# Output projection in one PSUM tile per output block, the state read ahead of the solve, and a longer fill behind one DMA round trip

## The chip, the cores and the metric

The kernel runs on one core of a Trainium2 chip. The metric is the device time of one launch, in microseconds: before the change three runs gave 1146.88, 1148.94 and 1152.93, median 1148.94. The engines are PE (matmul), DVE (vector), ACT (scalar), POOL, and SP, which only issues DMAs here. Each runs its own queue strictly in the order in which the program was laid down.

## The reference, cut to what matters

One decoder layer on 544 tokens (512 of a prompt, 32 of eight sample requests of four tokens), model width 1024, all in float32:

```
x = layer_norm(ALPHA*x + 0.5*swiglu(x, ffn1))
proj = x @ w_in                       # RWKV columns and convolution columns
r, k, v, decay, a, kk = f(proj)       # 8 heads of 64
S <- S diag(w) + (S(-kk))(kk*a)^T + v k^T ;  o = S r        # per token
y_rwkv = group_norm(o)... * g ;  y_conv = c_b * depthwise_conv(c_c*c_h)
x = layer_norm(ALPHA*x + concat(y_rwkv, y_conv) @ w_out)
x = layer_norm(ALPHA*x + 0.5*swiglu(x, ffn2))
```

Outputs are the two x parts, the new recurrence state and the shift and convolution states. `concat(y_rwkv, y_conv) @ w_out` is the output projection: 1024 inputs, in eight blocks of 128 (0 and 1: the first four heads, 2 and 3: the last four heads, 4 to 7: the convolution).

## The kernel before, in words

**Layout.** Activations lie transposed: features on the 128 partitions, tokens along the free axis, in halves h = 0 (tokens 0 to 255) and h = 1 (256 to 543). A large product is exact to nearly float32 by three fast products: each operand is split into a high part (ACT copies it, line 133) and a low part (DVE subtracts, line 134), and `mm3` issues high x high, high x low, low x high (lines 149 to 151), 256 or 288 columns each, into one PSUM tile named `mm`, of which there are three. The recurrence's small products are plain float32, 64 columns, into five PSUM tiles named `sm`.

**Weights.** `wload` takes a raw tile, issues its DMA on SP, and splits it into an `hl` tile. Raw and `hl` tiles come from rings in strict rotation. While the output projection runs, the `hl` ring has four slots (three of its own and one extra, `w4`), the raw ring two. A new load may be split into its slot only when the last matmul that reads the slot's earlier weights is done.

**Recurrence.** The heads form two groups, g = 0 and g = 1. Tokens go in eight chunks of 64. `elim(g)` inverts the chunks' small triangular matrices: DVE rounds on 16x16 blocks, a round trip through DRAM (tiles `De`, `Dd`, `DM`), then small matmuls (line 929). `chain(g)` then takes the eight chunks one after another. A step is: SC times the state S (line 977), copied to W by ACT (979); XT times W (984), copied to UV by DVE and ACT (985, 986); BK times UV (991), added into the next state by four DVE operations (1000, 1002); and the output, S times AR (1009) plus UV times SC (1013), both into one `sm` tile, copied to O by ACT (1015). `sample(g)` does the same for the sample tokens.

**What sets the order.** The critical work is a generator that yields a number where it must wait; `weave` then draws that many units (times a factor per stage, the table FILL) of background work from a queue `bg`: matmuls of other products. Then a list scheduler of the framework, with its own idea of durations, lays down each engine's queue. The order on the chip is fixed; a row that waits blocks all rows behind it on its engine.

**Around the change.** The fill of `elim(1)`, of `chain(1)` and of what follows is, in this order: the last convolution block (`conv_last`, weights `in_win`), the output projection's inputs 4 to 7, 0 and 1 for h = 0 (`wout(0)`, weights `wo_c` and `wo_0`), then inputs 2 and 3 (`last(0)`, weights `wo_1`). Then `wout(1)` and, behind it, `last(1)`; beside them run the group norm of the last heads and the layer norm of half 0 (`layer_norm`, lines 194 to 231), and then the second FFN starts.

Of the kernel before, what the change touches and what calls it, by code (L numbers as in the profile page):

```python
# [15 lines left out]
OP = mybir.AluOpType  # L16
# [5 lines left out]
KD = D // P  # L22
# [5 lines left out]
T = TP + NSEQ * TS  # L28
# [27 lines left out]
def R(par):  # L56
    return slice(64 * par, 64 * par + 64)
# [4 lines left out]
def body(ctx: ExitStack, tc: tile.TileContext, xT, gu1, wd1, win, wo_c, wo_0, wo_1, gu2, wd2, lora, w0, vec, cst,  # L62
         sst, cstate, s0, y_o, wkvp_o, wkvs_o, shift_o, conv_o):
    nc = tc.nc
    PE, ACT, DVE, POOL = nc.tensor, nc.scalar, nc.vector, nc.gpsimd
# [12 lines left out]
    xhl = keep.tile([P, 2, KD, T], F32R, name="xhl")  # L78
# [10 lines left out]
    def big():  # L89
        return ps.tile([P, 512], F32, name="mm", bufs=3)  # L90

    def sm():
        return ps.tile([P, 512], F32, name="sm", bufs=5)
# [15 lines left out]
    def wtiles():  # L109
        return raw_tile(), hl_tile()  # L110

    def wload(src, n=1024, parts=1):
        raw, hl = wtiles()
        m = n // parts
        for i in range(parts):
            dma(raw[:, i * m:i * m + m], src[:, i * m:i * m + m])
            wsplit(hl, raw, i * m, i * m + m)
        return hl
# [23 lines left out]
            hl, i = hl[i // 4], i % 4  # L142
        return hl[:, j, i * P:(i + 1) * P]

    def mm3(out, hl, src, ks, c0, c1, off=0):
        n = len(ks)
        for i, k in enumerate(ks):
            wh, wl = (block(hl, j, off + i) for j in range(2))
            PE.matmul(out, wh, src[:, 0, k, c0:c1], start=(i == 0), stop=False)  # L149
            PE.matmul(out, wh, src[:, 1, k, c0:c1], start=False, stop=False)  # L150
            PE.matmul(out, wl, src[:, 0, k, c0:c1], start=False, stop=(i == n - 1))  # L151
            if i % 2 and i < n - 1:
                yield 6 * ((c1 - c0) / 2.4 + 3)

    bg = deque()
# [467 lines left out]
    z = pool(zst, "zp").tile([P, KD, T], F32, name="z")  # L623
# [6 lines left out]
    raw, hl = wtiles()  # L630
# [244 lines left out]
    def elim(g, mid=None):  # L875
        AR = ARs[g]
        est = ExitStack()
        ep = pool(est, f"elim{g}")
        AT = ep.tile([P, 16, 16], F32, name="AT")
        De = ep.tile([P, 16, 16], F32, name="De")  # L880
        tm = ep.tile([P, 64], F32, name="tm")
        dma(AT, diag(Ad))
        POOL.memset(De, 0.0)
        POOL.memset(De.rearrange("p a b -> p (a b)")[:, 0:256:17], 1.0)
        for pl in range(2):
            for par in range(2):
                sc = SC[R(par), pl, par, 0:8, 0:64]
                DVE.tensor_tensor(sc, sc, offm[R(par), None, :].to_broadcast([64, 8, 64]), op=OP.mult)
        yield 3000
        for k in range(15):  # L890
            n = 15 - k
            tv = tm[:, :n * (k + 1)].rearrange("p (i j) -> p i j", j=k + 1)
            DVE.tensor_tensor(tv, AT[:, k, k + 1:16, None].to_broadcast([P, n, k + 1]),
                              De[:, k, None, 0:k + 1].to_broadcast([P, n, k + 1]), op=OP.mult)
            DVE.tensor_tensor(De[:, k + 1:16, 0:k + 1], De[:, k + 1:16, 0:k + 1], tv, op=OP.add)
            yield 400
        DVE.tensor_copy(AT, De.rearrange("p a b -> p b a"))
        dma(diag(Dd[0]), De)
        dma(diag(Dd[1]), AT)
        for d, x in zip(Dd, (DM[:, 0:8], DT)):  # L900
            for par in range(2):
                dma(x[R(par)].rearrange("p c d t -> p (c d) t"), d[par, :, 0:64].rearrange("c s t -> s c t"))
        est.close()
        if mid is not None:
            mid()
        yield 6000
        pieces = (range(0, 4), range(4, 8), range(8, 9))
        for rnd in range(4):
            for x in pieces:
                sam = x[0] == 8  # L910
                m = (64, 64, 32, 16)[rnd]
                j0 = (0, 16, 32, 48)[rnd]
                nn = (64, 48, 32, 16)[rnd]
                if sam:
                    m, j0, nn = 32, 0, 32
                q = sm()
                for c in x:
                    for pl in range(2):
                        for par in range(2):
                            r0 = 64 * par  # L920
                            pr = slice(r0, r0 + (32 if sam else 64))
                            o = ((c - x[0]) * 2 + pl) * nn
                            lhs = DM[pr, c, pl, 0:m] if rnd else SC[pr, pl, par, c, 0:m]
                            rhs = (DM if rnd == 0 else DT if rnd == 1 else XT) if not sam else XT
                            if sam and rnd < 2:
                                rhs = ident[pr, 0:32]
                            else:
                                rhs = rhs[pr, c, pl, j0:j0 + nn]
                            PE.matmul(q[r0:r0 + m, o:o + nn], lhs, rhs, start=True, stop=True)  # L929
                cc = slice(x[0], x[-1] + 1)  # L930
                qv = q[:, :2 * nn * len(x)].rearrange("p (c d t) -> p c d t", c=len(x), d=2)
                if rnd == 0:
                    for pr in (slice(0, 32), slice(64, 96)) if sam else (slice(0, P),):
                        ACT.activation(DM[pr, cc, :, 0:nn], qv[pr], AF.Copy)
                    yield 300
                    continue
                if rnd == 1 and not sam:
                    DVE.tensor_copy(XT[:, cc, :, 0:16], DT[:, cc, :, 0:16])
                    DVE.tensor_tensor(XT[:, cc, :, 16:64], qv, DT[:, cc, :, 16:64], op=OP.add)
                    yield 300  # L940
                    continue
                for par in range(2):
                    pr = slice(64 * par, 64 * par + m)
                    dst = XT[pr, cc, :, j0:j0 + nn]
                    if sam:
                        DVE.tensor_tensor(dst, qv[pr], ident[pr, None, None, 0:32].to_broadcast([32, 1, 2, 32]), op=OP.add)
                    elif par:
                        ACT.copy(dst, qv[pr])
                    else:
                        DVE.tensor_copy(dst, qv[pr])  # L950
                yield 300
            if rnd == 0:
                for pl in range(2):
                    for par in range(2):
                        POOL.tensor_copy(SC[R(par), pl, par, 0:8, 0:64], AR[R(par), pl, 0:8, 0, :])
# [4 lines left out]
    def chain(g, cp):  # L960
        S = Sn = None
        tl = cp.tile
        AR = ARs[g]
        for c in range(8):
# [5 lines left out]
            for pl in range(2):  # L970
                for par in range(2):
                    dst = q[R(par), pl * 64:pl * 64 + 64]
                    if c == 0:
                        o = R(1 - par)
# [3 lines left out]
            W = tl([P, 2, 64], F32, name="W", bufs=2)  # L978
            ACT.activation(W, v2(q), AF.Copy)
            yield 1000  # L980
            q = sm()
            for pl in range(2):
                for par in range(2):
# [5 lines left out]
            for pl in range(2):  # L989
                for par in range(2):  # L990
                    PE.matmul(q[R(par), pl * 64:pl * 64 + 64], BK[:, pl, par, c, :], UV[:, pl, par, c, :],
                              start=True, stop=True)
# [3 lines left out]
            for par in range(2):  # L996
                dst = Sn[R(par), :, par, :] if c < 7 else SF[R(par)]
                src = v2(q, R(par))
                if c:
                    DVE.tensor_tensor(dst, S[R(par), :, par, :], src, op=OP.add)  # L1000
                    src = dst
                DVE.tensor_tensor(dst, src, pe[R(par)], op=OP.mult)
            if c == 7:
                dma(wkvp_o[:, 2 * g:2 * g + 2, :], SF)
            q2 = sm()
            if c:
                for pl in range(2):
                    for par in range(2):
                        PE.matmul(q2[R(par), pl * 64:pl * 64 + 64], S[R(par), pl, par, :], AR[R(par), pl, c, 1, :],
                                  start=(pl == 0), stop=False, skip_group_check=True)  # L1010
            for pl in range(2):
                for par in range(2):
                    PE.matmul(q2[R(par), pl * 64:pl * 64 + 64], UV[:, pl, par, c, :], SC[:, pl, par, c, 64:128],
                              start=(c == 0), stop=True, skip_group_check=True)
            ACT.activation(O[:, :, c, :], v2(q2), AF.Copy)
            S = Sn
# [212 lines left out]
    z = pool(ctx, "zp2", "right").tile([P, KD, T], F32, name="z")  # L1229
# [13 lines left out]
    def ysplit(k, y, c0, c1):  # L1243
        split(xhl[:, 0, k, c0:c1], xhl[:, 1, k, c0:c1], y[:, c0:c1])
# [22 lines left out]
    def wout(h):  # L1267
        c0, c1 = HALF[h]
        if h == 0:
            ys = [(k, yload(k)) for k in (0, 1)]  # L1270
            for k in range(KD):
                ACT.activation(z[:, k], z[:, k], AF.Identity, scale=ALPHA, bias=rb[:, k:k + 1])
        for src, n, ks in ((wo_c, 2, (4, 5, 6, 7)), (wo_0, 4, (0, 1))):
            for m in range(KD // n):
                if h == 0 and n == 2 and m == 2:
                    for k, y in ys:
                        ysplit(k, y, 0, T)
                w = wload(src[m])
                for d in range(n * m, n * m + n):
                    o = big()  # L1280
                    yield from mm3(o[:, :c1 - c0], w, xhl, ks, c0, c1, (d - n * m) * len(ks))
                    zz = z[:, d, c0:c1]
                    DVE.tensor_tensor(zz, zz, o[:, :c1 - c0], op=OP.add)
                    yield 6 * 120

    def last(h):
        c0, c1 = HALF[h]
# [132 lines left out]
```

## Time and profile before

| | |
|---|---|
| runs | 1146.88, 1148.94, 1152.93 us |
| the profiled execution, its own time | 1144.4 us |
| its span, first to last instruction | 1142.3 us |
| mean granted PE clock | 0.992 |
| PE, DVE, ACT, POOL busy | 1106.8, 857.2, 586.1, 174.2 us |
| elim(1) up to its first matmul | about 601 to 629 us of the span |
| chain(1) | about 648 to 703 us |
| wout(1) and last(1) | about 712 to 749 us |

PE is busy for 97% of the span, but a busy PE is not a full one: matmuls are pipelined, each is shown with its whole latency (some 0.3 us), and consecutive ones start 0.12 to 0.13 us apart where nothing disturbs them. What a stage of PE work costs is therefore read from starts, and from the waits.

### The profile page before, as it was taken

Reading aid. Unit: us, or ns where it says so; the run is one execution under the profiler, and the core shown is the slowest. Engines: PE = TensorE matmul, PEld = TensorE weight load, DVE = VectorE, ACT = ScalarE, POOL = GpSimd, SP = SyncE. Lnnn points to the kernel's source line nnn. Section 1 sums busy time; section 2 is a strip of 40 time slices with the busy share of each in tenths; the row PEclk is TensorE's granted clock in tenths of the full one; section 3 lists DMA queues with packets and bytes.
Section 4 is the critical chain, followed back from the end, with each engine's and each line's share of the span. In section 5 each row is a group of like instructions: output and inputs, shape, how many; then the busy total and the mean of one; then the engine's idle time right before and its main releaser. Section 6 shows DMA issues by size and latency. Waiting matters only on the chain.

```text
span 1142.3 us, 22932 instructions
## 1 busy us (share of the span) xinstructions
PE 1106.8 (97%) x9300; PEld 1049.3 (92%) x9300; DVE 857.2 (75%) x1602; ACT 586.1 (51%) x1066; POOL 174.2 (15%) x282
## 2 busy tenths in 40 slices
PE   8999999999999999999999999899999999999995
PEld 7999999999999999898788878899999999999995
DVE  7677988879776867745577368988979888787755
ACT  6545555564553476553245343657555555545523
POOL 0021131312100032221011100001222212121000
PEclk9999999999999999999999999999999999999998
DMA  8557594957742242262128423353675949577302
GB/s 281 119 112 168 131 219 116 200 149 166 163 145 78 92 132 66 53 121 78 48 66 223 118 76 96 130 184 63 130 180 124 228 97 217 148 161 167 105 1 79
DMA packets 97626, 149.32 MB, mean 131 GB/s; under 512 B 35056, under 2 KB 58992, under 8 KB 97520
## 3 DMA queue, kind: packets, MB, share of 16 engines
q1 hardware_dynamic: 70320, 111.67, 32.3%
q0 software_dynamic: 27200, 36.18, 20.2%
q8 instruction: 73, 1.20, 0.4%
q14 instruction: 33, 0.27, 0.1%
HBM read 129.17 MB, written 9.75 MB: 122 GB/s over the span
## 4 chain that ended last, share of the span: by engine, by line
PE 68%; DMA 10%; DVE 10%; issue 7%; ACT 5%; SPq 0%; ACTq 0%; POOL 0%; POOLq 0%; DVEq 0%
PE mm L149 7%; PE mm L464 7%; PE mm L151 7%; PE mm L465 6%; PE mm L466 6%; PE mm L150 6%; DMA raw<-in_gu 6%; PE sm L464 5%; PE sm L466 5%; PE sm L465 5%; DVE hl L134 2%; ACT hl L133 2%; PE sm L929 1%; DMA z<-in_xT 1%; PE sm L208 1%
## 5 line engine op out<-in xcount | busy, mean ns | idle before, releaser
L134 DVE TENSOR_TENSOR hl<-raw,hl 128x1024 fp32r<-128x1024 f32 (+3 forms) x228 | 269.5, 1189 | 67.0 <-ACT hl L133 64.8
L133 ACT ACTIVATE hl<-raw 128x1024 fp32r<-128x1024 f32 (+3 forms) x228 | 231.5, 1027 | 86.2 <-DVE raw L431 32.5
L149 PE MATMUL mm<-xhl,hl 128*128 128x256 f32 (+1 forms) x768 | 235.6, 307 | 8.4 <-ACT xhl L137 4.9
L151 PE MATMUL mm<-xhl,hl 128*128 128x256 f32 (+1 forms) x768 | 227.8, 298 | 1.4 <-DVE hl L134 1.4
L150 PE MATMUL mm<-xhl,hl 128*128 128x256 f32 (+1 forms) x768 | 226.4, 295 | 0.6 <-DVE xhl L231 0.3
L149 PEld LDWEIGHTS mm<-xhl,hl 128*128 128x128 f32 x768 | 147.4, 192 | 16.6 <-ACT xhl L137 5.2
L150 PEld LDWEIGHTS mm<-xhl,hl 128*128 128x128 f32 x768 | 147.5, 192 | 6.5 <-issue 1.6
L151 PEld LDWEIGHTS mm<-xhl,hl 128*128 128x128 f32 x768 | 147.0, 192 | 5.8 <-DVE hl L134 2.4
L464 PE MATMUL sm<-xhl,hl 128*128 128x272 f32 x432 | 124.7, 289 | 0.0
L466 PE MATMUL sm<-xhl,hl 128*128 128x272 f32 x432 | 124.6, 289 | 0.0
L465 PE MATMUL sm<-xhl,hl 128*128 128x272 f32 x432 | 124.6, 288 | 0.0
L464 PE MATMUL mm<-tv,hl 128*128 128x272 f32 x288 | 83.7, 291 | 3.5 <-ACT cpb L525 2.9
L466 PE MATMUL mm<-tv,hl 128*128 128x272 f32 x288 | 83.6, 290 | 0.0
L465 PE MATMUL mm<-tv,hl 128*128 128x272 f32 x288 | 82.5, 286 | 0.0
L466 PEld LDWEIGHTS sm<-xhl,hl 128*128 128x128 f32 x432 | 81.6, 189 | 0.0
L443 POOL DMA_DIRECT2D raw<-in_wd x32 | 39.3, 1494 | 277.2 <-DVE hlb L138 275.4
L465 PEld LDWEIGHTS sm<-xhl,hl 128*128 128x128 f32 x432 | 81.3, 188 | 0.0
L464 PEld LDWEIGHTS sm<-xhl,hl 128*128 128x128 f32 x432 | 81.3, 188 | 0.0
L437 POOL DMA_DIRECT2D raw<-in_gu x36 | 43.4, 1206 | 238.4 <-DVE hlb L138 131.7
L464 PEld LDWEIGHTS mm<-tv,hl 128*128 128x128 f32 x288 | 54.1, 188 | 5.0 <-ACT cpb L525 3.5
L464 PE MATMUL mm<-hhl,hl 128*128 128x272 f32 x192 | 57.0, 302 | 1.7 <-ACT sv L570 1.6
L464 PE MATMUL sm<-hhl,hl 128*128 128x272 f32 x192 | 55.9, 291 | 0.0
(367 smaller groups left out, 2818.9 us busy)
## 6 DMA issues: line engine op xcount, KB each, us to landing
raw<-in_gu SPq DMA_DIRECT2D x86, 512.0 KB, 5.0
raw<-in_gu POOLq DMA_DIRECT2D x36, 512.0 KB, 7.4
raw<-in_wd SPq DMA_DIRECT2D x32, 512.0 KB, 4.8
raw<-in_win SPq DMA_DIRECT2D x26, 512.0 KB, 3.6
raw<-in_wd POOLq DMA_DIRECT2D x32, 256.0 KB, 6.5
raw<-in_wd SPq DMA_DIRECT2D x16, 384.0 KB, 3.3
z<-cpb POOLq DMA_DIRECT2D x16, 272.0 KB, 8.7
z<-sv POOLq DMA_DIRECT2D x16, 272.0 KB, 5.7
```

Source lines behind the costliest of these rows:

```text
L133: ACT.activation(hl[:, 0, a:b], raw[:, a:b], AF.Copy)
L134: DVE.tensor_tensor(hl[:, 1, a:b], raw[:, a:b], hl[:, 0, a:b].bitcast(F32), op=OP.subtract)
L149: PE.matmul(out, wh, src[:, 0, k, c0:c1], start=(i == 0), stop=False)
L150: PE.matmul(out, wh, src[:, 1, k, c0:c1], start=False, stop=False)
L151: PE.matmul(out, wl, src[:, 0, k, c0:c1], start=False, stop=(i == n - 1))
L208: PE.matmul(v[:, :n], ones, qq[:, i, :], start=(j == 0 and i == 0), stop=(j == 3 and i == 1))
L437: POOL.dma_start(x.rearrange("p (s c) -> p s c", s=2), bass.AP(tensor=a11.tensor, offset=a11.offset, ap=[[2 * D, P], [P * 2 * D, 2], [1, 5 ...
L443: POOL.dma_start(four(x)[:, i], bass.AP(tensor=a11.tensor, offset=a11.offset, ap=[[DFF, P], [P * DFF, 2], [1, 256]]), accum_op=OP.add)
L464: PE.matmul(out, wh, src(0, i), start=(first and i == 0), stop=False, skip_group_check=True)
L465: PE.matmul(out, wh, src(1, i), start=False, stop=False, skip_group_check=True)
L466: PE.matmul(out, wl, src(0, i), start=False, stop=(i == n - 1), skip_group_check=True)
L929: PE.matmul(q[r0:r0 + m, o:o + nn], lhs, rhs, start=True, stop=True)
```

## The change

Three edits.

1. In `chain`, the four products S times AR of a step stand ahead of XT times W, and their `sm` tile is taken there. Before, they stood behind the state update.
2. In `wout`, one PSUM tile per output block d takes the convolution inputs (12 matmuls) and inputs 0 and 1 (6 matmuls); before, they were two groups in two passes over d, each with a DVE addition into z. The weights are loaded in the order wo_0[0], wo_c[0], wo_c[1], wo_0[1], wo_c[2], wo_c[3]; before, the four wo_c came first. The splits of inputs 0 and 1 stand ahead of all products; before, in the middle. `mm3` gets arguments that leave the accumulation open, and then also yields behind its last pair.
3. In `elim`, the wait behind the round trip through DRAM draws 15000 units for g = 1; before, 6000. The stage's factor is 0.392.

```diff
-    def mm3(out, hl, src, ks, c0, c1, off=0):
+    def mm3(out, hl, src, ks, c0, c1, off=0, start=True, stop=True):
...
-            PE.matmul(out, wh, src[:, 0, k, c0:c1], start=(i == 0), stop=False)
+            PE.matmul(out, wh, src[:, 0, k, c0:c1], start=(start and i == 0), stop=False)
...
-            PE.matmul(out, wl, src[:, 0, k, c0:c1], start=False, stop=(i == n - 1))
-            if i % 2 and i < n - 1:
+            PE.matmul(out, wl, src[:, 0, k, c0:c1], start=False, stop=(stop and i == n - 1))
+            if i % 2 and not (stop and i == n - 1):
                 yield 6 * ((c1 - c0) / 2.4 + 3)
...
-        yield 6000
+        yield 15000 if g else 6000
...
             ACT.activation(W, v2(q), AF.Copy)
             yield 1000
+            q2 = sm()
+            if c:
+                for pl in range(2):
+                    for par in range(2):
+                        PE.matmul(q2[R(par), pl * 64:pl * 64 + 64], S[R(par), pl, par, :], AR[R(par), pl, c, 1, :],
+                                  start=(pl == 0), stop=False, skip_group_check=True)
             q = sm()
...
-            q2 = sm()
-            if c:
-                for pl in range(2):
-                    for par in range(2):
-                        PE.matmul(q2[R(par), pl * 64:pl * 64 + 64], S[R(par), pl, par, :], AR[R(par), pl, c, 1, :],
-                                  start=(pl == 0), stop=False, skip_group_check=True)
...
-        for src, n, ks in ((wo_c, 2, (4, 5, 6, 7)), (wo_0, 4, (0, 1))):
-            for m in range(KD // n):
-                if h == 0 and n == 2 and m == 2:
-                    for k, y in ys:
-                        ysplit(k, y, 0, T)
-                w = wload(src[m])
-                for d in range(n * m, n * m + n):
-                    o = big()
-                    yield from mm3(o[:, :c1 - c0], w, xhl, ks, c0, c1, (d - n * m) * len(ks))
-                    zz = z[:, d, c0:c1]
-                    DVE.tensor_tensor(zz, zz, o[:, :c1 - c0], op=OP.add)
-                    yield 6 * 120
+            for k, y in ys:
+                ysplit(k, y, 0, T)
+        n = c1 - c0
+        for d in range(KD):
+            if d % 4 == 0:
+                w0 = wload(wo_0[d // 4])
+            if d % 2 == 0:
+                wc = wload(wo_c[d // 2])
+            o = big()
+            yield from mm3(o[:, :n], wc, xhl, (4, 5, 6, 7), c0, c1, (d % 2) * 4, stop=False)
+            yield from mm3(o[:, :n], w0, xhl, (0, 1), c0, c1, (d % 4) * 2, start=False)
+            zz = z[:, d, c0:c1]
+            DVE.tensor_tensor(zz, zz, o[:, :n], op=OP.add)
+            yield 6 * 120
```

What the change makes of the queues is shown at the three places of which the prediction speaks. Line numbers from 985 on are up to six higher in the changed kernel: 984, 991, 1000, 1002 and 1009 before are 990, 997, 1006, 1008 and 985 now; 1283 (the addition into z) is 1285, 1294 is 1296.

**PE where elim(1) waits for its round trip.** DM is the tile that the DRAM round trip fills; the wide rows (lines 149 to 151) are fill. Before:

```order
L150 MATMUL mm<-xhl,hl 128x256
L929 MATMUL sm<-DM,SC 64x64 x2
L929 MATMUL sm<-cs,SC 32x32 x4
L151 MATMUL mm<-xhl,hl 128x256
L149 MATMUL mm<-xhl,hl 128x256
```

Now:

```order
L151 MATMUL mm<-xhl,hl 128x256
L929 MATMUL sm<-DM,SC 64x64
L149 MATMUL mm<-xhl,hl 128x256
L150 MATMUL mm<-xhl,hl 128x256
L151 MATMUL mm<-xhl,hl 128x256
L149 MATMUL mm<-xhl,hl 128x256
L150 MATMUL mm<-xhl,hl 128x256
L151 MATMUL mm<-xhl,hl 128x256
L929 MATMUL sm<-DM,SC 64x64
L149 MATMUL mm<-xhl,hl 128x288
L929 MATMUL sm<-DM,SC 64x64 x30
```

The run of 256-column fill ahead of the first row that reads DM has 26 matmuls before and 42 now, and six more stand between the two rows that wait for the two halves of DM. From the first line-929 row to the first of chain(1) there are 6 runs of fill before and 14 now; in chain(0) 28 before and 24 now, in chain(1) 35 and 33; from the start of chain(0) to the layer norm of half 0, 87 and 89.

**PE in a step of chain(0)**, one piece of the difference (S and AR name this step's two operands of the moved product):

```order
 L151 MATMUL mm<-xhl,hl 128x288
 L977 MATMUL sm<-S,SC 64x64
-L149 MATMUL mm<-xhl,hl 128x288
+L985 MATMUL sm<-AR_4703,S 64x64
 L977 MATMUL sm<-S,SC 64x64 x3
-L150 MATMUL mm<-xhl,hl 128x288
-L151 MATMUL mm<-xhl,hl 128x288
-L149 MATMUL mm<-xhl,hl 128x288
-L984 MATMUL sm<-W,XT 64x64 x4
```

The moved product takes the place of a single fill matmul between the first row of line 977 and the three others.

**PE and ACT in wout(1), at the step from output block 3 to 4.** hl_8385 is wo_0[0], hl_8532 is wo_c[2]; mm_8492 and mm_8536 are the PSUM tiles of blocks 3 and 4. PE now:

```order
L151 MATMUL mm_8492<-xhl_68,hl_8385 128x288
L149 MATMUL mm_8536<-xhl_68,hl_8532 128x288 [waits Activation_49]
L150 MATMUL mm_8536<-xhl_68,hl_8532 128x288
L151 MATMUL mm_8536<-xhl_68,hl_8532 128x288 [waits DVE_49]
L149 MATMUL mm_8536<-xhl_68,hl_8532 128x288
```

ACT now (hl_8527 is wo_0[1], hl_8589 is wo_c[3], lnr the layer norm's square root):

```order
L133 ACTIVATE hl_8527<-raw_8526 128x1024 [waits DMAHW2_49]
L1098 ACTIVATE gq1_8380<-gq1_8380 128x288 [waits Activation_49]
L137 ACTIVATE xhl_68<-O_4697 128x288 [waits DVE_49]
L133 ACTIVATE hl_8532<-raw_8531 128x1024 [waits DMAHW3_49,PE_49]
L137 ACTIVATE xhl_68<-O_4697 128x288 [waits DVE_49]
L133 ACTIVATE hl_8589<-raw_8588 128x1024 [waits DMAHW4_49]
L218 ACT_TABLE_LOAD
L218 ACTIVATE lnr_7089<-sm_8512,eps_69 128x256 [waits PE_49]
```

wo_c[2] is the fifth load and so falls into the slot of the first, wo_0[0], which block 3 still reads; its split waits for PE, and PE's next row waits for the split. Before, the fifth load was wo_0[0] and its slot held wo_c[0], read last in block 1.

## The prediction, on record before the result

> **What bounds the kernel now.** I read the page's chain of waits first, then PE's waits, then the stretches in which the granted clock falls, then PE, ACT and DVE in order of time around the edits.
>
> ```profile
> span 1142.3 us, 22932 instructions
> PE 1106.8 (97%) x9300; PEld 1049.3 (92%) x9300; DVE 857.2 (75%) x1602; ACT 586.1 (51%) x1066; POOL 174.2 (15%) x282
> PE 68%; DMA 10%; DVE 10%; issue 7%; ACT 5%; SPq 0%; ACTq 0%; POOL 0%; POOLq 0%; DVEq 0%
> ```
>
> PE is the bound nearly everywhere, so fill that only moves from one place to another changes nothing; an edit counts by the PE time that it empties or fills. PE's waits, by releaser, whole span, then 700 to 760 us alone (us in total, times, longest):
>
> ```profile
> PE sm L929 <- DMA DM<-Dd: 2.3, 1, 2.3
> ...
> PE mm L149 <- DVE z L1283: 1.9, 2, 1.4
> PE mm L149 <- ACT hl L133: 0.9, 1, 0.9
> PE mm L151 <- DVE hl L134: 0.6, 1, 0.6
> ```
>
> The first is the round trip of elim(1), the other three (3.4 us) are wout(1) and last(1). Each place is followed by a stretch at half clock, whose rows show PE, PEld, DVE, ACT and POOL busy, then the granted clock:
>
> ```profile
> 626.50:629.10 2.60, 0.34 (x3) 0.13 (x2) 0.04 (x1) 0.38 (x1) 2.12 (x8) 1.00 1.26 201
> 629.80:633.25 3.45, 3.45 (x18) 3.45 (x17) 0.00 (x0) 0.43 (x2) 0.00 (x0) 0.51 1.28 241
> 736.80:742.40 5.60, 3.12 (x19) 2.35 (x18) 5.60 (x13) 2.60 (x5) 0.00 (x0) 1.00 0.00 0
> 742.50:745.90 3.40, 3.40 (x17) 3.40 (x16) 2.08 (x5) 0.36 (x1) 0.00 (x0) 0.50 0.79 257
> ```
>
> 3.4 us at half clock does 1.7 us of work, so each costs 1.7 us. In both cases some 2 us of idle came just before. The third thing to see is that changing between fill and small products costs:
>
> ```profile
> 608.63 0.29 PE L151 MATMUL mm<-xhl,hl 128*128 128x288 f32 x1
> 608.76 0.30 PE L149 MATMUL mm<-xhl,hl 128*128 128x288 f32 x1
> ...
> 656.25 0.28 PE L150 MATMUL mm<-xhl,hl 128*128 128x256 f32 x1
> 656.47 0.33 PE L977 MATMUL sm<-S,SC 128*64 128x64 f32 x2
> 656.73 0.38 PE L151 MATMUL mm<-xhl,hl 128*128 128x256 f32 x1
> 657.04 0.45 PE L977 MATMUL sm<-S,SC 128*64 128x64 f32 x6
> ```
>
> Undisturbed fill starts every 0.13 us (288 columns; 0.12 for 256). From 656.25 to 657.04 stand two fills, worth 0.24, and two small records at about 0.05: 0.34 of work in 0.79 us, with two changes to small and one back. I take 0.3 us for a run of fill between small products.
>
> **Edit 3, the longer fill.** Now 42 instead of 26 fills of 256 columns stand ahead of the first row that reads DM: 16 x 0.12 = 1.9 us more. The wait was 2.3. DVE's last rows ahead of the round trip now leave two fill operations behind themselves:
>
> ```profile
> 619.12 0.41 DVE L1153 TENSOR_TENSOR cu<-cc,mm 128x256 f32<-128x256 f32 x1
> 619.45 0.18 DVE L1155 TENSOR_TENSOR cu<-cc,mm 128x32 f32<-128x32 f32 x1
> 619.55 0.17 DVE L895 TENSOR_TENSOR De<-De,tm 128x15 f32<-128x15 f32 x1
> ```
>
> That brings De forward by some 0.4 us. 1.9 + 0.4 covers the 2.3: **-2.3** (bounds -1.9 and -2.5), and the half clock behind it goes: **-1.7** (bounds 0 and -1.7). What is late next is nothing: the six fills between the two waiting rows cover the second half of DM. If the fill were gone, the wait would be back whole.
>
> The Trainium skill (TensorE: Matmul & The Clock Gate, Part 1: The HAM clock gate) says that the clock falls after at least one idle window of about 3.4 us and comes back after a busy one. The trace agrees on the length of the slow stretch, 3.4 us, and differs on its cause: 2.3 us of wait was enough. By the page's rule the wait would not explain the half clock, and -1.7 would be 0.
>
> **Edit 1, the moved product.** No instruction is added: 28 matmuls per group move. They wait for S, as line 977 does, so no new wait; queued behind them on PE is XT times W, which waits for ACT's W anyway:
>
> ```profile
> 657.58 0.28 ACT L979 ACTIVATE W<-sm 128x128 f32<-128x128 f32 x1 [1.16 <-PE sm L977]
> ```
>
> Four of them (0.4 us, eight records at 0.05) fit into W's 0.3 us and its handover. Their `sm` tile is held one solve longer, with five tiles for it; I cost that at nothing, and at most at one drain of 0.3 us per step, 2 us, if the tiles run out. What counts is the runs of fill: 4 fewer in chain(0), 2 fewer in chain(1), 8 more in the small products of elim(1), 2 more in all around: +2 x 0.3 = **+0.6** (bounds -1.8, the chains' alone, and +2.4, elim's alone).
>
> **Edit 2, the DVE additions.** Sixteen additions of about 0.37 us (the spacing behind the 0.4 us that a row shows) leave DVE:
>
> ```profile
> L1283 DVE TENSOR_TENSOR z<-z,mm 128x288 f32<-128x288 f32 x16 | 7.1, 446 | 0.7 <-PE mm L151 0.7
> L134 DVE TENSOR_TENSOR hl<-raw,hl 128x1024 fp32r<-128x1024 f32 x7 | 8.4, 1218 | 0.0
> ```
>
> In wout(0) they lie beside PE's work and are worth nothing. In wout(1) they are the 1.9 us of PSUM waits: a tile lasts 18 fills (2.4 us) instead of 6 (0.8), and DVE's lag no longer reaches PE. The 0.9 is of the same sort, since DVE was held by ACT, which was held by a load:
>
> ```profile
> 731.76 1.06 ACT L133 ACTIVATE hl<-raw 128x1024 fp32r<-128x1024 f32 x1 [1.33 <-DMA raw<-in_wo]
> ...
> 733.25 0.48 DVE L231 SCALAR_TENSOR_TENSOR xhl<-z,vc,xhl 128x256 fp32r<-128x256 f32 x1 [1.00 <-ACT xhl L230]
> 733.65 0.45 DVE L1283 TENSOR_TENSOR z<-z,mm 128x288 f32<-128x288 f32 x1
> ```
>
> So the tail's 3.4 us of waits go: **-3.4**, and its half clock with them, -1.7.
>
> **Edit 2, the ring.** Here a wait is added. wo_c[2] takes the slot of wo_0[0], read until block 3 ends, and block 4 needs it at once. PE stands for ACT's split and its handover, less what two matmuls on the high part cover, then for DVE's low part: 0.3 of drain + 1.06 + 1.22 - 0.3 = **+2.3** in wout(1) (bounds 1.1, the high part alone, and 2.6). In wout(0) the same split stands in ACT's queue ahead of the chain's UV copy, and PE has only the rows behind that copy left: 1.06 + 0.26 + 0.2 = **+1.5** (bounds 0.3, if other rows cover all but the copy, and 2.6). How such a split delays the copy shows already:
>
> ```profile
> 695.85 1.06 ACT L133 ACTIVATE hl<-raw 128x1024 fp32r<-128x1024 f32 x1 [2.31 <-PE mm L151]
> 696.93 0.26 ACT L986 COPY UV<-sm 64x128 f32<-64x128 f32 x1
> ```
>
> Behind the split in wout(1) are queued another split, a table load and the layer norm's root:
>
> ```profile
> 724.97 1.28 ACT L218 ACT_TABLE_LOAD   x1
> 726.28 0.48 ACT L218 ACTIVATE lnr<-sm,eps 128x256 f32<-128x256 f32 x1
> 727.44 1.74 DVE L219 RECIPROCAL lnr<-lnr 128x256 f32<-128x256 f32 x1
> ```
>
> The root moves from 0.4 to some 5 us behind the variance sums, and all of DVE's normalizing (16 operations at 0.4, the reciprocal, five additions) stands ahead of the low split of last(1)'s first weights. Added up from these rows, that split ends 15.7 us behind the variance sums; PE, with 84 fills at 0.13 and the 2.3 us stall, arrives at 13. PE has 6 fills for the difference: **+1.9** (bounds 0 and 3). I expect one stall of the three to bring a half clock: **+1.7** (bounds 0 and 5.1); two earlier waits of 0.9 and 0.6 brought none by themselves.
>
> **Edit 2, the input splits.** Lines 1240 and 137 move ahead. Splits of y stand in ACT's queue ahead of a W copy, behind a transfer:
>
> ```profile
> y<-ycd SPq DMA_DIRECT2D x2, 272.0 KB, 3.1
> 673.29 0.64 ACT L137 ACTIVATE xhl<-y 128x544 fp32r<-128x544 f32 x1
> ```
>
> Issue to landing 3.1 plus two splits is 4.4 us; PE has about 4.8 us of rows (12 fills, 24 small records, the 512-column sample product, three changes) until it needs W: **0** (bounds 0 and 1.4, a slow landing). Nor does SP delay them: the weight load ahead finds its raw tile free.
>
> **Sum.** -2.3 - 1.7 + 0.6 - 3.4 - 1.7 + 2.3 + 1.5 + 1.9 + 1.7 = **-1.1 us**, against the profiled execution: span 1142.3 to 1141.2, its own time 1144.4 to 1143.3. That execution lies 4.5 us under the median of the three runs, 1148.94; the sum applied to it gives **1147.8**. A measurement of this kernel tells some 0.5% (5.7 us) from no change: the forecast is no change.
>
> **Rivals.**
>
> *The waits go and none comes* (faster). If the ring's splits are covered, the sum is -2.3 - 1.7 + 0.6 - 3.4 - 1.7 = -8.5, 1140.4. For it: every wait named is in the rows, and ACT is idle half the time. Against it: block 4 needs the slot that block 3 has just read, and no row stands between.
>
> *The ring's stalls bring half clock each* (slower). Where each of the three stalls empties PE for 1.5 us or more inside one of the clock's windows, all three pay 1.7, 3.4 more than in the sum, and with the upper bounds of the two ring stalls (2.6 each, +1.4) and of last(1) (3, +1.1) the result is -1.1 + 3.4 + 1.4 + 1.1 = +4.8, 1153.7; it is slower than before as soon as two stalls do. For it: 2 us of idle did so twice. Against it: 0.9 did not.
>
> *Half clock has nothing to do with the waits* (the page's rule). Both slow stretches stay and none is added: -1.7 is struck twice and +1.7 once, -1.1 + 3.4 - 1.7 = +0.6, 1149.5. For it: nothing but two stretches are there to judge by. Against it: each stands right behind the idle.
>
> *The longer fill does nothing*, since the fills wait for their own weights or DVE is late: 4.0 us are not won, +2.9, 1151.8. Against it: PE is dense up to 626.5.
>
> **How the numbers follow.** Chances: the forecast 0.52, all covered 0.20, stalls with half clock 0.12, clock apart 0.08, fill idle 0.08. The forecast's own range is 1143 to 1152. The whole range takes in the covered case and the slower one, **1140 to 1153.5**. Faster by over 0.5% (under 1143.2): the covered case and a little of the forecast, 0.24. Slower by over 0.5% (above 1154.7): the upper half of the slower case and part of the idle fill, 0.09. Within: 0.67.
>
> **What would show it.** Right: PE's wait for DM under 0.4 us with clock 1.00 behind it; PSUM waits on the addition gone; PE waiting for ACT L133 and DVE L134 at block 4, 1 to 2.6 us each; the root some 5 us behind the variance sums. Wrong: no PE wait at block 4 (the ring is covered, faster), or a wait for DM that stays.

## The result, and the profile after

Four runs of the changed kernel took 1130.86 to 1137.86 us, median **1134.97 us**; four runs of the kernel before beside them had a median of 1147.91. The ratio is **0.9884, 95% interval 0.9849 to 0.9919**: faster by 1.2%, where the prediction said no change (1147.8) and its range ended at 1140.

The page of the changed kernel, in the lines that answer to those of before:

```profile
span 1134.5 us, 22909 instructions
PE 1099.5 (97%) x9300; PEld 1045.3 (92%) x9300; DVE 851.6 (75%) x1586; ACT 586.2 (52%) x1066; POOL 172.6 (15%) x282
PE 64%; DVE 11%; DMA 10%; issue 9%; ACT 5%; POOL 0%; SPq 0%; ACTq 0%; POOLq 0%; DVEq 0%
```

PE is the bound as before. PE's waits of the changed kernel at the places of which the prediction spoke, out of the list for the whole span (us in total, times, longest):

```profile
PE mm L151 <- DVE hl L134: 1.4, 2, 0.8
PE mm L149 <- DVE z L1285: 0.9, 1, 0.9
PE sm L929 <- DMA DM<-Dd: 0.5, 2, 0.3
PE mm L149 <- DVE z L1296: 0.5, 1, 0.5
...
PE mm L149 <- ACT hl L133: 0.2, 1, 0.2
```

The wait for DM fell from 2.3 to 0.5 us, and the tail's waits are about 2 us (0.9, 0.6 of line 151's 1.4, 0.5). No row shows the two stalls at output block 4 that the prediction added.

Waits alone don't make 13 us. Two quantities worked out from trace and runs are used from here on. **Time beside the fill** of a stage is its elapsed time less what its fill would take undisturbed (0.1325 us per fill of 288 columns, 0.1185 per fill of 256, the spacing of such rows); it doesn't change when fill only moves from one stage to another. **At full clock** means less the time lost to half clock: for a stage half the length of the half-clock stretches in it, for a run span times mean granted clock. In us, beside the fill and at full clock, one profile of each kernel:

| stage | before | edit 1 alone | edit 2 alone | edit 3 alone | all three |
|---|---|---|---|---|---|
| chain(0) | 30.5 | 27.5 | 30.5 | 30.5 | 27.5 |
| elim(1) up to the first row that reads DM | 17.9 | 14.9 | 18.1 | 16.3 | 13.6 |
| elim(1)'s small products behind it | 9.8 | 9.7 | 9.6 | 11.6 | 12.1 |
| chain(1) | 32.8 | 30.5 | 32.6 | 30.4 | 31.4 |
| tail: variance sums of half 0 to layer norm of half 1 | 6.7 | 6.7 | 6.0 | 6.5 | 4.9 |
| the rest of the region | 12.1 | 11.8 | 12.1 | 11.7 | 11.5 |

The first two columns and the last say where time was saved: in the steps of chain(0), whose only edit is the moved product, in elim(1) up to DM, and in chain(1). The prediction gave this edit +0.6. Differences of half a microsecond are not to be read: two profiles of the changed kernel differ by up to 0.6 in a stage.

For the stages as the view of stretches shows them, chain(0), the head of elim(1), chain(1) and the tail, before and then with edit 1 alone (window, length, then PE, PEld, DVE, ACT, POOL busy, granted clock, DMA share, GB/s):

```profile
525.30:569.10 43.80, 43.80 (x505) 33.19 (x506) 21.36 (x57) 9.82 (x31) 3.31 (x12) 1.00 0.18 62
579.90:589.80 9.90, 9.66 (x92) 7.97 (x91) 7.28 (x17) 2.83 (x8) 0.71 (x4) 1.00 0.39 102
651.40:703.40 52.00, 52.00 (x571) 40.63 (x571) 36.89 (x90) 21.46 (x52) 3.21 (x10) 1.00 0.27 84
724.40:750.20 25.80, 22.29 (x142) 20.69 (x141) 22.94 (x49) 12.57 (x19) 0.00 (x0) 0.93 0.42 143
```

```profile
526.50:566.10 39.60, 39.24 (x496) 30.83 (x495) 21.53 (x56) 10.63 (x31) 3.29 (x12) 1.00 0.19 60
577.50:585.40 7.90, 7.34 (x93) 6.34 (x92) 7.40 (x16) 2.78 (x8) 0.70 (x4) 1.00 0.39 81
646.30:696.10 49.80, 49.66 (x572) 38.77 (x571) 36.28 (x89) 21.68 (x52) 3.19 (x10) 1.00 0.28 87
716.90:740.90 24.00, 20.70 (x142) 19.12 (x140) 22.78 (x49) 12.22 (x18) 0.00 (x0) 1.00 0.45 154
```

Chain(0) is 4.2 us shorter with 11 fills less in it (1.4 us of fill that went elsewhere); PE is busy all of the 43.8 us before, so no list of waits could show this.

### The profile page after: what moved, and what is told of

It reads as the page before. It is cut to its first block, busy times and chain, and to the rows that moved or that the text cites. A ratio compares the mean times of both kernels' runs of the same rounds, so it can differ in the third digit from the quotient of the medians.

```text
span 1134.5 us, 22909 instructions
## 1 busy us (share of the span) xinstructions
PE 1099.5 (97%) x9300; PEld 1045.3 (92%) x9300; DVE 851.6 (75%) x1586; ACT 586.2 (52%) x1066; POOL 172.6 (15%) x282
## 4 chain that ended last, share of the span: by engine, by line
PE 64%; DVE 11%; DMA 10%; issue 9%; ACT 5%; POOL 0%; SPq 0%; ACTq 0%; POOLq 0%; DVEq 0%
PE mm L149 7%; PE mm L464 7%; PE mm L466 6%; PE mm L465 6%; PE mm L151 6%; PE mm L150 6%; DMA raw<-in_gu 5%; PE sm L464 4%; PE sm L466 4%; PE sm L465 4%; DVE hl L134 3%; ACT hl L133 2%; PE sm L929 1%; DMA raw<-in_wd 1%; PE sm L208 1%
```

## The experiments

All twelve kernels were timed in five rounds, four to a comparison, each against the kernel before in the same comparison. Means at full clock (span times mean granted clock), and the time lost to half clock, with twice the standard error:

| kernel | runs | ratio, 95% interval | at full clock, us | lost to half clock, us |
|---|---|---|---|---|
| before, three comparisons | 68 | | 1135.5 ± 0.5 | 13.0 ± 1.0 |
| edit 1 | 6 | 0.9889 (0.9853 to 0.9926) | 1127.9 ± 1.5 | 7.8 ± 2.1 |
| edit 2 | 12 | 0.9980 (0.9952 to 1.0009) | 1134.6 ± 1.1 | 11.5 ± 2.4 |
| edit 3 | 12 | 0.9939 (0.9917 to 0.9962) | 1134.3 ± 1.1 | 8.5 ± 1.2 |
| edits 1 and 2 | 12 | 0.9904 (0.9875 to 0.9934) | 1127.8 ± 0.5 | 10.4 ± 2.4 |
| edits 1 and 3 | 6 | 0.9911 (0.9889 to 0.9934) | 1126.2 ± 0.9 | 10.6 ± 2.3 |
| edits 2 and 3 | 11 | 0.9916 (0.9889 to 0.9942) | 1132.9 ± 0.8 | 7.4 ± 1.6 |
| all three, with the first comparison | 10 | 0.9879 (0.9844 to 0.9914) | 1126.5 ± 1.3 | 7.3 ± 1.6 |
| ring forced | 6 | 0.9861 (0.9824 to 0.9897) | 1124.8 ± 1.6 | 7.9 ± 1.2 |
| before, grouped | 12 | 1.0003 (0.9982 to 1.0024) | 1135.1 ± 0.7 | 11.7 ± 2.0 |
| all three, apart | 12 | 1.0037 (1.0011 to 1.0062) | 1142.7 ± 1.1 | 8.6 ± 3.0 |
| all three, prefetch | 6 | 0.9896 (0.9872 to 0.9920) | 1126.6 ± 1.3 | 8.5 ± 1.7 |
| all three, blocks | 6 | 0.9885 (0.9852 to 0.9918) | 1124.8 ± 1.2 | 10.2 ± 1.7 |

The ratio of "all three" is that of the later comparison alone. Of the last column, 2.4 to 4.0 us lie behind the last matmul in every profile and cost nothing, so only its differences count.

### The edits one by one

Edit 1 alone:

```diff
+            q2 = sm()                      # S times AR, ahead of XT times W
...
             for pl in range(2): ... PE.matmul(q[...], XT[R(par), c, pl, :], W[R(par), pl, :], ...)
...
-            q2 = sm()                      # ... no longer behind the state update
```

> Only the moved product S times AR (edit 1). In the two profiled executions the time that PE spends beside its wide fill (elapsed time of a stage less 0.13 us for each fill of 288 columns and 0.12 for each of 256) fell from 30.5 to 27.5 us in chain(0) and from 32.8 to 31.4 in chain(1). Theory A, changes of shape: it is edit 1 that does this, since a step's rows of 64x64 stand between rows of 128x64 less often; -3 to -5 us against before, chain(0) rest 27.5 +- 0.7, with the two waits of elim(1) and the tail still there. Theory B, the waits alone: edit 1 is worth what the prediction gave it, between -1.8 and +2.4 us; the 3 us in chain(0) came from the other edits' order, and this run's chain(0) rest stays near 30.5.

Measured: ratio 0.9889, at full clock 8.3 us under the before of the same comparison (1136.2). Chain(0) has the 27.5 us of theory A to the tenth; chain(1) is 30.5, less than expected, and elim(1) up to DM, which no theory had named, is 3.0 us shorter. Theory B falls; theory A has the right stage, and its -3 to -5 in all is too little. Edit 1 alone is worth most of what the change is worth.

Edit 2 alone (the hunks on `mm3` and `wout`), and edit 3 alone:

```diff
-        yield 6000
+        yield 15000 if g else 6000
```

> Only the output projection in one PSUM tile (edit 2). Theory A: the ring costs nothing, as in the changed kernel's trace, and the tail wins 3.5 us there; -3 to -5 us against before, no PE wait for ACT line 133 or DVE line 134 between output blocks 3 and 4; the PE wait for DM (2.3 us) stays. Theory B, the prediction's sum for this edit: -3.4 - 1.7 + 2.3 + 1.5 + 1.9 + 1.7 = +2.3 us.

> Only the longer fill behind elim(1)'s round trip (edit 3). Theory A: the wait for DM falls from 2.3 to about 0.4 us and no half clock stands behind it: -2 to -4 us, of which some is given back by the additional runs of fill between elim's small products (85 fills in 22.2 us before, 22.9 after with the half clock gone). Theory B: the wait shrinks only when all three edits stand together; -1 to +1 us.

Measured for edit 2: 0.9980, an interval that holds 1; at full clock -1.6 ± 1.4 against its comparison. The wait for DM stayed (2.6), as theory A said. At full clock the gain is under its -3 to -5, which the plain ratio's interval (-5.5 to +1.0 us) doesn't rule out; +2.3 (theory B) is out. Its PE waits from 700 to 765 us show why it is so small:

```profile
PE mm L151 <- DVE hl L134: 2.2, 1, 2.2
PE mm L149 <- DVE z L1285: 0.6, 1, 0.6
PE mm L149 <- ACT hl L133: 0.4, 1, 0.4
```

The waits for the PSUM additions went from 1.9 to 0.6, and the low split of last(1)'s first weights became 2.2 us late. That is the size of the prediction's +1.9, but not its path: the layer norm's root starts 1.4 us behind the variance sums (730.62 against 729.21), not 5. DVE's last normalizing, ahead of the low split, waited 3.05 us for ACT's rows of line 230, and ACT stood 5.23 us for a load (raw from in_gu) ahead of them.

Measured for edit 3: 0.9939; at full clock -1.9 ± 1.4, theory A's -2 to -4 within the error; the plain ratio says some -7 us, half clock included. The wait for DM is 0.8, not 0.4. It saves 1.6 us up to DM (17.9 to 16.3), and gives 1.8 back in the small products behind (9.8 to 11.6), which have 15 runs of fill among them instead of 7. The last is inside the prediction's bounds (+2.4 for these 8 runs). Chain(1) is 2.4 us shorter, which neither theory named; in program order it has 8 runs of fill fewer, 27 instead of 35. The half clock in elim's small products is gone, but this profile has one at the start of chain(1) instead (656.2 us).

### Pairs

> Edits 1 and 3 without edit 2. Over the first five comparisons, span times mean granted clock (so that stretches at half clock don't count) was, as the mean of the runs: before 1136.2, edit 1 alone 1127.9 (-8.3), edit 2 alone 1134.6 (-1.6), edit 3 alone 1134.3 (-1.9), all three 1125.3 (-10.9). Theory A, the three add: -8.3 - 1.9 = -10.2 at full clock, 1126, and 0.988 to 0.991 in the plain ratio. Theory B, edit 2 is needed for the other two to be worth all they show: -8 or less at full clock.

> Edits 1 and 2 without the longer fill. Theory A: -8.3 - 1.6 = -9.9 us at full clock; the wait for DM stands at about 1.7 us as with edit 1 alone. Theory B, overlap: -8 to -8.8.

> Edits 2 and 3 without the moved product. Theory A: -1.6 - 1.9 = -3.5 us at full clock; the two chains have 27 and 27 runs of fill and 32 and 28 direct changes of shape, against 23 and 32, 19 and 12 of the changed kernel. Theory B, the prediction's sum without its +0.6 for edit 1: -1.7 us.

> The changed kernel as it is, beside the three others of this comparison. From the single edits, in span times mean granted clock (edit 1 -8.3 us, edit 2 -1.6, edit 3 -1.9): theory A, they add, -11 to -12.5 against before. Theory B, what edit 2 and edit 3 win is the same waits that edit 1 shortens already: -8 to -9, as edits 1 and 3 together showed (-8.4).

The edits of these kernels are the hunks of the change that their names give. Measured at full clock, each against the before of its own comparison: edits 1 and 3 -8.4, edits 1 and 2 -7.8, edits 2 and 3 -2.7, all three -8.3. Without edit 1, edits 2 and 3 are worth 1.6 to 2.7 us; on top of it, within the error, nothing: theory B holds for the pairs with edit 1, and -2.7 ± 1.2 lies between the two theories for edits 2 and 3. Why the gains don't add stays open. The expectation of -11 to -12.5 for all three was wrong; the first four runs (1125.3) had been a little low. What is left of the gain in plain time, about 5 us, is less time at half clock (13.0 to 7.3). In plain time the shares are less clear: by their ratios edit 1 alone is worth some 13 us, edits 2 and 3 together some 10, all three some 14. Edits 2 and 3 get most of theirs from half clock (14.2 to 7.4 in their comparison), edit 1 from full clock.

### The ring, forced into the slot that the prediction named

One line ahead of the loop over d in `wout` puts wo_0[0] into the extra slot, which holds one tile; wo_c[2], four loads later, must follow into it:

```diff
         n = c1 - c0
+        wstate["hl"] += (3 - wstate["hl"]) % 4
         for d in range(KD):
```

> The changed kernel with one line more: before each wout the count of the weight ring is advanced so that wo_0[0] takes the extra slot, which holds one tile only; so wo_c[2], four loads later, must take wo_0[0]'s slot, as the prediction said it did. Theory A, the slot was misread but the price was right: the prediction's stalls of 2.3 us in wout(1) and 1.5 in wout(0) appear, with a half clock of 1.7 behind at least one; +3.8 to +7 us against the changed kernel, ratio to before 0.992 to 0.995. Theory B, such a split is covered whatever slot it takes: within 1 us of the changed kernel, ratio 0.988.

In the changed kernel the slot is another. The built program gives wo_0[0] the address 76992, and wo_c[1] and wo_c[2] both 85184: the pool hands out the slot that came free first, not the one that was given out first. In wout(0), too, wo_c[2] follows wo_c[1] (68800) and not wo_0[0] (85184). So the strict rotation in the description of the kernel doesn't hold for the three own slots of the `hl` ring; in the kernel before, both rules give the same slots. PE, ACT and DVE of the changed kernel at this place:

```profile
716.33 0.29 PE L151 MATMUL mm<-xhl,hl 128*128 128x288 f32 x1
716.46 1.89 PE L216 MATMUL sm<-lnq,ones 128*128 128x256 f32 x8
718.00 0.48 PE L149 MATMUL mm<-xhl,hl 128*128 128x288 f32 x1
...
718.84 0.29 PE L151 MATMUL mm<-xhl,hl 128*128 128x288 f32 x1
718.97 0.30 PE L149 MATMUL mm<-xhl,hl 128*128 128x288 f32 x1
```

```profile
716.66 1.06 ACT L133 ACTIVATE hl<-raw 128x1024 fp32r<-128x1024 f32 x1 [1.03 <-PE mm L151]
```

```profile
717.75 1.23 DVE L134 TENSOR_TENSOR hl<-raw,hl 128x1024 fp32r<-128x1024 f32 x1 [0.45 <-ACT hl L133]
```

The row at 716.33 is block 3's last on wo_c[1]. wo_c[2] is split right behind it, while PE works on the variance sums (line 216) and block 3's six rows on wo_0[0] (718.00 to 718.84); block 4 starts at 718.97 and needs the low part at its third row. Nothing waits. Forced, PE's waits from 700 to 760 us are:

```profile
PE mm L149 <- ACT hl L133: 2.0, 1, 2.0
PE mm L151 <- DVE hl L134: 1.4, 1, 1.4
PE mm L149 <- DVE z L1286: 0.2, 1, 0.2
```

So the stall in wout(1) has the predicted size, 2.0 us where 2.3 was said; in wout(0) none appears. Yet the kernel is as fast as the changed one, 0.9861. At full clock the tail is 1.6 us longer (6.5 against 4.9 beside the fill) and chain(1) 1.4 shorter (30.0 against 31.4; the scheduler, with another slot, laid three runs of fill fewer). In plain time this profile's tail is 3.3 us longer (25.6 against 22.3), for a half clock follows the stall. Both theories fall in part: the mechanism and its price in wout(1) are real, a loss of 3.8 to 7 us in all is not. Where the runs win the tail's loss back is shown only for chain(1)'s 1.4. The misread slot alone doesn't explain the miss.

### What edit 1 changes: the price of a change of shape

A step of chain(0) on PE, before:

```profile
533.30 0.30 PE L150 MATMUL mm<-xhl,hl 128*128 128x288 f32 x1
533.52 0.33 PE L991 MATMUL sm<-UV,BK 128*64 128x64 f32 x2
533.78 0.32 PE L1009 MATMUL sm<-AR,S 64*64 64x64 f32 x2
534.04 0.45 PE L991 MATMUL sm<-UV,BK 128*64 128x64 f32 x6
534.41 0.44 PE L1009 MATMUL sm<-AR,S 64*64 64x64 f32 x6
534.78 0.45 PE L1013 MATMUL sm<-SC,UV 128*64 128x64 f32 x8
```

Behind the operation stands the shape of the weights, 128*64 or 64*64. Six records of one shape and the change to the next take 0.37 us, two records and the change 0.26; so a record is 0.03 to 0.05 and a **change of shape 0.16 to 0.2 us**. Before, S times AR (64*64) stands in pieces between products of 128*64; moved, it stands beside XT times W, which is 64*64 too. Two kernels test this.

The first keeps the four S times AR together, in the old place:

```diff
-  PE.matmul(q[...], BK[:, pl, par, c, :], UV[...], ...)
+  bk = PE.matmul(q[...], BK[:, pl, par, c, :], UV[...], ...)
...
-  PE.matmul(q2[...], S[R(par), pl, par, :], AR[...], ...)
+  m = PE.matmul(q2[...], S[R(par), pl, par, :], AR[...], ...)
+  after(m, bk)      # behind the last BK times UV on PE, no semaphore
```

> The kernel before, with S times AR left in its place behind the state's update product, but all four of a step held together behind all four of BK times UV (an order on PE without a semaphore). The trace of the kernel with edit 1 alone fits 0.35 us for each run of fill between small products and 0.12 us for each direct change between small products of 128 rows of contraction and of 64. Here the two chains have 13 and 5 changes fewer than before, and 7 and 5 runs of fill more. Theory A, the price list of runs and changes: -18 x 0.12 + 12 x 0.35 = +2.0 us in the two chains. Theory B, what counts is that S times AR no longer stands in pieces between BK times UV, on whose result the next step waits: the chains win as with edit 1 alone, -3 to -5 us.

Measured: 1.0003. Chain(0) stays at 30.4 beside the fill, chain(1) goes from 32.8 to 33.5. Theory A's +2.0 is too high for the +0.6 in the stages and the +0.5 ± 0.9 of the runs; with the prices fitted later (0.26 and 0.16) the same counts give +0.2. Theory B's gain didn't come, but the 12 runs of fill that the scheduler laid into the room, 3.1 us at 0.26, could hide it, so this kernel alone doesn't decide. The next one does.

The second keeps S times AR ahead of XT times W, as edit 1 put it, but lays it in between the products SC times S, one by one:

```diff
-  PE.matmul(dst, SC[:, pl, par, c, 0:64], S[...], ...)
+  m = PE.matmul(dst, SC[:, pl, par, c, 0:64], S[...], ...)
+  if ar is not None: after(m, ar)
+  ar = PE.matmul(q2[...], S[R(par), pl, par, :], AR[...], ...)
+  after(ar, m)
```

> The changed kernel, with the four S times SC and the four S times AR of each step made to alternate one by one. Nothing is added. In the two chains the direct changes between 128 and 64 rows go from 19 and 12 to 60 and 58, the runs of fill from 23 and 32 to 25 and 27. Theory A, the price list (0.12 and 0.35 us): 87 x 0.12 - 3 x 0.35 = +9.4 us against the changed kernel, some 1144 to 1145. Theory B, edit 1 wins by its place in the step alone: within 2 us of the changed kernel.

```profile
533.75 0.33 PE L979 MATMUL sm<-S,SC 128*64 128x64 f32 x2
534.01 0.32 PE L982 MATMUL sm<-AR,S 64*64 64x64 f32 x2
534.27 0.33 PE L979 MATMUL sm<-S,SC 128*64 128x64 f32 x2
534.52 0.33 PE L982 MATMUL sm<-AR,S 64*64 64x64 f32 x2
```

Measured: 1.0037, slower than the kernel before although the moved product still stands ahead of the solve and the update; at full clock 16 us over the changed kernel. Two records and a change take 0.26 us, 0.16 of it the change. The chains are 8.9 and, at full clock, 5.0 us longer beside the fill: 13.9, which is 87 changes at 0.16. Theory A holds with 0.16 for its 0.12; theory B falls. The order also makes W later, but PE's waits show none of it: between 520 and 730 us they come to 1.5 us, none of them on a row of the chains. So the same products cost 16 us more or less by their order, 13.9 of it in the chains.

### Two attempts to go further

```diff
+            if h and d == 6:
+                ahead.append(wload(wo_1[0]))
...
-                w = wload(wo_1[d // 4])
+                w = ahead.pop() if ahead else wload(wo_1[d // 4])
```

> The changed kernel, with the load and split of last(1)'s first weights called for ahead of output block 6 of wout(1), so that both splits stand ahead of the layer norm's last operations on ACT and DVE. Theory A, the tail's remaining 2 us are DVE's queue: the waits of PE at the start of last(1) (0.9, 0.6 and 0.5 us) fall to under 0.7 in all, the stretch from the variance sums to the next layer norm from 22.3 to about 21 us; -1 to -1.5 us, too little for a clear ratio. Theory B, DVE's normalizing only moves and the wait comes back at the additions into z: the stretch stays within 0.4 us of 22.3.

Measured: 0.9896. The tail's waits are 1.0 (line 151, low split) and 0.9 (addition into z), about 2 us as before; its time beside the fill 5.1 against 4.9. Theory B holds, and what it gave as the reason fits: DVE has the same work to do there, and only what comes late changes.

In `elim`, for g = 1, the waits of 300 behind each group become one per round:

```diff
-                    yield 300
+                    yield (5400 if sam else 0) if g else 300
```

> The changed kernel, with the fill inside elim(1)'s small products drawn once per round (four blocks of about 18 fills) instead of after each of the twelve groups. Runs of fill there go from 15 to 7, in chain(1) from 32 to 29. Theory A, the price list, which by a fit over the stages of all runs so far is 0.26 us for a run of fill and 0.16 for a direct change: -8 x 0.26 - 3 x 0.26 = -2.9 us against the changed kernel at full clock. Theory B, the small products then wait for their copies by ACT and DVE, which the fill between the groups covered: PE waits of 0.3 us and more on line 929 come back, and the gain is under 1 us.

Measured: 0.9885; at full clock 1124.8 ± 1.2, against 1127.4 ± 1.1 of the changed kernel in the same comparison. The small products behind DM take 9.5 us beside the fill instead of 11.5, chain(1) 30.4 instead of 31.0, and no PE wait is listed from 600 to 660 us. That is theory A in the stages; in plain time the two can't be told apart (medians 1136.53 and 1136.02), since these runs lost 3 us more to half clock. No version clearly beat the changed kernel.

## Why the prediction was wrong, point by point

**Edit 1, "+0.6": this step failed, and at full clock it is most of the miss.** The prediction said that "what counts is the runs of fill" and priced these alone, at 0.3 us. (Its sum also counted the 8 runs that edit 3 brings.) A fit over the chain stages of all runs, made after the first eight, gives 0.26 for a run, near it, and 0.16 for a direct change between small products of 128*64 and 64*64, which it left out; single stages lie up to some 1.5 us off the fit. In program order edit 1 alone takes 4 and 1 runs and 13 and 16 changes out of the two chains: 5 x 0.26 + 29 x 0.16 = 5.9 us; measured 3.0 + 2.3 = 5.3. The rows were in the trace of before: in the step shown above two records of 64*64 take 0.26 us, and eight of one shape in a row 0.38. A look at which shapes the moved rows come to stand between would have shown it. The Trainium skill (TensorEngine Tiling (Array Packing), Tiling Modes) states that a change of tiling mode drains TensorE; the trace agrees that a change costs time, 0.16 us, and doesn't show that it is a drain. A further 3.0 us fell in elim(1) up to DM, whose order also changed, and which the prediction didn't price: the head (the rows of lines 837 to 869) goes from 10.0 to 7.9 us, and the wait for DM from 2.3 to 1.7. What made the head shorter is not shown. It has 3 runs of fill instead of 5, which at 0.26 is 0.5 us of the 2.1, and over the whole stage the counts don't differ: 16 runs in both kernels, 30 and 31 changes. Alone the edit is worth -8.3 ± 1.7 us at full clock.

**Edit 2, the ring, "+2.3" and "+1.5": wrong.** The step that failed is the statement, also in the part on the change, that the fifth load falls into the slot of the first. It was read from the code's count; the pool gives the slot that is free first. The named sign for "wrong", no PE wait at block 4, is what the trace shows. Forced, its price was right in wout(1) (2.0 of 2.3) and wrong in wout(0), where no wait appeared for the +1.5.

**Edit 2, the additions, "-3.4", and last(1), "+1.9": right in size.** Together they leave 1.9 us of the tail's 3.4 us of waits; in the changed kernel some 2.1 are left, with edit 2 alone 3.2. The PSUM waits went from 1.9 to 0.6, as said. The late low split is partly luck: the root stood 2.4 us behind the variance sums in the changed kernel (720.72 against 718.35) and 1.4 with edit 2 alone, not 5, and no stall of 2.3 us held PE back.

**Edit 3, "-2.3" and its half clock, "-1.7": right in kind.** The wait went to 0.8 alone and 0.5 in the changed kernel, where under 0.4 was said. The half clock in elim(1)'s small products stands in all five profiles with the short fill (before, edit 1, edit 2, edits 1 and 2, grouped) and in none of the nine with the long one. But it is in part only moved: six of these nine have a half clock near the start of chain(1), between 651 and 663 us, against one of the five.

**Half clock, net "-1.7": too small.** The runs lost 13.0 us before and 7.3 after, 5.7 ± 1.9 less. Five kernels with the short fill lost 10.9 in the mean, eight with the long one 8.6, so some 2.3 of the 5.7 may hang on edit 3; edit 1 alone, with the short fill, lost only 7.8. Where the rest comes from can't be told from one profile of each kernel; it stays open.

**The rivals.** The covered case (1140.4) had the right sign and no stall from the ring (though for another reason: the slot was another, not the split covered), but gave edit 1 the same +0.6. That its -8.5 is near the -8.3 at full clock is luck: it is the sum of what edits 2 and 3 were to win, which at full clock added nothing to edit 1. No rival gave the moved product more than its bound of -1.8; the range ended where it did for this one term.

## What to carry to other kernels

Where PE is dense and works on small products, count the changes of weight shape in its order, between small products too and not only against the fill: here each cost 0.16 us, and no list of waits showed them. An edit that moves one product beside another of its shape won 8 us of 1136, some 5 of them where these changes fell away; the rest is not traced to a cause. Compare stages by their time beside the fill and at full clock; both remove scatter that the plain medians keep. And a rotation of buffers is read from the addresses of the built program, not from the count in the code.

## What the runs showed of the hardware

The granted clock is set for stretches of 3.413 us on a fixed grid within a run. Over the fourteen profiles, from 60 us to the last layer norm and leaving out stretches already at half clock, the columns that PE's matmuls passed in a stretch tell what follows: undisturbed fill passes 7,400. Of some 60 stretches with fewer than 3,100 columns, some 40 were followed by one at half clock, and nearly all of those with under 2,460; of some 4,200 with more than 3,100, none. A wait is not needed: 11 of the 60 have no gap between matmul starts above 0.4 us, and 5 of these were followed by half clock. The changed kernel in the later comparison shows one at the start of chain(1), where nothing waits:

```profile
644.50:647.90 3.40, 3.40 (x37) 2.95 (x35) 2.70 (x10) 2.03 (x6) 0.00 (x0) 1.00 0.86 255
647.90:651.30 3.40, 3.40 (x90) 3.17 (x91) 1.50 (x5) 0.81 (x4) 0.00 (x0) 1.00 0.15 58
651.35:654.70 3.35, 3.35 (x32) 2.84 (x28) 0.58 (x2) 1.08 (x4) 0.00 (x0) 0.50 0.00 0
```

PE is busy through the second stretch, with 90 matmuls, nearly all of them small (3,008 columns). So half clock follows low use of PE, by a wait or by small products, and between 2,460 and 3,100 columns not each time. Where a wait falls on the grid counts: the tail's waits of 1.35 and 0.61 us are the same before and with edit 1 alone. Before, both fell into one stretch, which passed 2,304 columns and was followed by half clock; with edit 1 alone they fell into two, which passed 3,168 and 6,048, and none followed.
